# Ordering each engine's instructions by a simulation with DMA queues and semaphores in time: a two-layer hybrid diffusion block

## The chip, the cores and the metric

One NeuronCore of a Trainium2 chip. TensorE (PE) multiplies, VectorE (DVE) and ScalarE (ACT) do the elementwise work, GpSimd (POOL) a little of it, and SyncE (SP) issues most of the loads. Each engine has its own instruction stream and takes it in the order in which it was written; an instruction whose operand is not there waits, and with it all that stands behind it on its engine. The metric is the device time of one execution in microseconds; the span of the profiled execution runs from its first to its last instruction.

## What is computed

Two layers act on 256 tokens `x` and 256 context tokens `ctx`, with 1024 features. In each, a half feed-forward block, a mixer and another half feed-forward block are added to the residual stream, all modulated by vectors made from `c` and `c_ctx`. All is in float32.

```python
def half_ffn(h, shift, scale, gate, g, wi, wo):
    return h + 0.5 * gate * swiglu(modulate(rms_norm(h, g), shift, scale), wi, wo)

def hybrid_layer(x, ctx, c, c_ctx, p, last):
    mod_x = (jax.nn.silu(c) @ p['ada_w'] + p['ada_b'])[:, None, :]
    ...
    x = half_ffn(x, sx[0], sx[1], sx[2], p['ffn1_norm'], p['ffn1_wi'], p['ffn1_wo'])
    ctx = half_ffn(ctx, sc[0], sc[1], sc[2], p['ffn1_norm'], p['ffn1_wi'], p['ffn1_wo'])
    u_x = modulate(rms_norm(x, p['mix_norm']), sx[3], sx[4]) @ p['w_in']
    ...
    x = x + sx[5] * mix_tokens(u_x, rows, dirs_x, states_x, p)
    x = half_ffn(x, sx[6], sx[7], sx[8], p['ffn2_norm'], p['ffn2_wi'], p['ffn2_wo'])
    if not last:
        ctx = ctx + sc[5] * mix_tokens(u_c, None, dirs_c, states_c, p)
        ctx = half_ffn(ctx, sc[6], sc[7], sc[8], p['ffn2_norm'], p['ffn2_wi'], p['ffn2_wo'])
    return x, ctx
```

`mix_tokens` joins four mixers (pooling, a long convolution by transforms, a gated linear attention with chunks, a gated short convolution) and multiplies by `w_out`. After two layers `x` is normalized once more.

## The kernel before, in words

Features lie on the 128 partitions in eight tiles `x` of 128 x 512 (256 tokens of `x`, 256 of `ctx`); the second layer's last stages run on 256 tokens alone. TensorE multiplies fp32 values as pairs of a rounded high part and a remainder: `split` (L171, L172) makes them, the cast to the high part on ScalarE (`whi` of a weight, `yh` of a normed input, `ah` of a modulation weight), the subtraction that gives the low part on VectorE (`wlo`, `yl`, `al`). `mm3` makes three matmuls of each product (L183 high by high, L184 and L185 high by low).

Three places matter below.

*The modulation vectors at the start.* `ada_pe` takes a slab of 512 columns of `ada_w` in eight pieces `adaw`; some go in as they are (L301), some are split into `ah` and `al` (L298, L299). The sums are copied into `row` by ScalarE (L303), turned by four small matmuls against `sum4` (L306), and written to `mods` by VectorE (L308); L366 makes `gs` of them. The first feed-forward block needs shift and scale, four slabs for eight feature tiles: tiles 0 to 3 need the first two slabs that come in, tiles 4 to 7 the other two. Its first two weight tiles are `whi_599`/`wlo_600` and `whi_607`/`wlo_608`; its normed inputs are `yh_519` to `yh_526`.

*The end of each feed-forward block and mixer, where a norm follows* (`project`, `part`). The last two output tiles are computed one half of the tokens after the other. As soon as the first half is done, `rstd` turns its sums of squares by four small matmuls (L406, L407), `rsqrt_cols` works out 1/rms in about fifteen tiny VectorE steps (L210, L212, L215 and three rounds of L219 and L221), and `bcast` spreads it over the partitions (two `diag` on VectorE, L231; two matmuls, L233). Meanwhile TensorE does the last two parts on the second half of the tokens; VectorE adds each to the residual tiles `x_22` and `x_23` (L487), and ScalarE squares them (L389, summed at L393). Then `norm` makes, tile by tile, `ny` (L427), `yh` (ScalarE, L430) and `yl` (L431), which the next block's first matmuls take. This stands four times in the program with 512 tokens: at 420, 628, 996 and 1370 us of the profiled execution.

*The mixer of the second layer*, at 1405 to 1440 us, where many small steps of four mixers are interleaved by a string of letters (`ORDERS`).

The order of the work is not that in which the program is written. The tile framework records all instructions with priorities, which the program shifts for single pieces (`prio`, `issue_after`), and a scheduler then lays them out engine by engine, going by the priorities and a simulation of when each is ready. Buffers are limited: 2 of `whi` and of `wlo`, 3 of `raw`, 4 PSUM buffers each of `psm` and `psa`, so a split also waits for the matmuls that still read its buffer.

Of the kernel before, what the change touches and what calls it, by code (L numbers as in the profile page):

```python
# [17 lines left out]
P = 128  # L18
# [11 lines left out]
CF = 136  # L30
# [30 lines left out]
class Builder:  # L61
# [58 lines left out]
    def mark(self, *engines):  # L120
        """The last instructions traced for VectorE and for the loads, or for other engines."""
        engines = engines or (mybir.EngineType.DVE, mybir.EngineType.SP)
        found = {}
        for i in reversed(self.nc.cur_bb.bb.instructions):
            if i.engine in engines and i.engine not in found:
                found[i.engine] = i
                if len(found) == len(engines):
                    break
        return found
# [23 lines left out]
    def warm_up(self):  # L153
        """Keeps TensorE busy until its first operands are there: its clock is halved after idling."""
        ps = self.pa((P, P))
# [18 lines left out]
    def stack(self, dst, src, low):  # L174
        """src [96, n], the same rows three times -> the high parts, but for one of the three, which gets the low parts: two
        such stacks, with the low parts in different places, make a product of 32 rows in one pass."""
        self.nc.scalar.copy(dst, src)
        s = slice(32 * low, 32 * low + 32)
# [27 lines left out]
    def rsqrt_cols(self, ps, n):  # L206
        """ps [P, n, 2]: v and -v/2. One after the other column by column, so that the columns' chains overlap."""
# [17 lines left out]
    def bcast(self, r, ntile):  # L225
        """r [tokens, ntile] per token -> PSUM [128, ntile*128], the same on every partition."""
# [47 lines left out]
    def ada_fetch(self, l, slab, pools):  # L274
        """The weights of a slab, by k."""
# [12 lines left out]
    def ada_pe(self, l, slab, ws, split):  # L288
        """The rows of c and c_ctx times the weights: four rows, each vector as its high and its low part, times both
        parts of the weights, for the last split parts of the inner dimension; as it is for the first."""  # L290
# [20 lines left out]
    def ada_group(self, l, chunks, vecs):  # L311
        """Yields after each piece of work."""
# [72 lines left out]
    def sumsq(self, m, lo, n):  # L385
        """Adds the squares of tokens lo..lo+n of feature tile m."""
# [11 lines left out]
    def rstd(self, lo, n):  # L398
        """Each token's 1/rms, tokens on partitions."""
# [11 lines left out]
    def spread(self, lo, r):  # L411
        """The same on every partition."""
# [21 lines left out]
    def scaled(self, l, name):  # L434
        """x times the norm's weights and scale, for products that begin before the norm's factor is there."""
# [18 lines left out]
    def project(self, m, wh, wl, act, gate, T, last):  # L454
        """x[m] += gate * (weights.T @ act); with last, the squares for the norm that follows.
        The last two tiles go one half of the tokens after the other, so that the norm of the first half
        can begin early."""
# [38 lines left out]
    def ffn(self, l, name, T, fill, last=1):  # L496
# [26 lines left out]
        def shifted(w):  # L523
            """What the norm's shift adds, per feature."""
# [14 lines left out]
        def late_act(w, c, rb):  # L539
            """act, for products that the norm's factor and shift are still to be applied to."""  # L540
# [65 lines left out]
    def spectra(self, l):  # L606
        """Yields after each piece of work."""
        nc, t = self.nc, self.t
        # the two halves of the positions lie on the two halves of the partitions
# [77 lines left out]
    def mirror(self, lo, hi, even, odd, i):  # L687
        """The transform (0: cosines, 1: sines) at frequencies f and 255 - f, out of the sums over the even and the odd
        positions: cos and sin at 255 - f are (-1)^n cos and -(-1)^n sin at f."""
# [9 lines left out]
    def mix(self, l, last):  # L699
# [8 lines left out]
        def fm(wg, c, n, TT, lo=0):  # L708
            """Features on partitions: n columns of the group for tokens lo..TT."""
# [24 lines left out]
        def tm(wg, tt):  # L734
            """Tokens on partitions, all columns of the group."""
# [29 lines left out]
        def conv_in():  # L765
            """Conformer convolution: the gated input, positions on partitions."""
# [73 lines left out]
        # output projection  # L840
# [16 lines left out]
    def conv(self, l, cv, nq):  # L857
        """The depthwise convolution by a transform of length 2 * CF (at odd multiples of half its frequency, so that the
        CF frequencies are alike), which the positions and half the taps fit in; then norm and SiLU. The first 128
        frequencies lie on partitions, the CF - 128 further ones at first on the free axis."""  # L860
# [10 lines left out]
        # the filter's transform  # L871
# [12 lines left out]
        # the input's transform, and the product  # L884
# [55 lines left out]
        n = T // P  # L940
# [11 lines left out]
    def hyena(self, l, uc, nq, marks):  # L952
# [13 lines left out]
        def tok(pair):  # L966
            """Positions on partitions, the even ones and the odd ones."""
# [15 lines left out]
        for o in range(2):  # L983
            # at f and at 255 - f: the transform, and its product with the filter's
# [22 lines left out]
            # back: what the cosines and the sines at f weigh for the even positions, and for the odd ones  # L1007
# [54 lines left out]
    def gla(self, l, kk, gg, qq, vv, nq):  # L1062
# [71 lines left out]
        # states: chunk index 0..3 for x, 4..7 for ctx  # L1134
# [28 lines left out]
    def gla_gate(self, l, nq, rr):  # L1163
        """The norm over each head's values, and the gate."""
# [30 lines left out]
    def gla_read(self, seq, ke, qbd, vv, before, blk):  # L1195
# [5 lines left out]
        for cp in range(2):  # L1201
            tt = seq * 2 + cp
            # scores within each chunk: its positions on half of the partitions
# [29 lines left out]
    def finish(self):  # L1233
        """The last norm, with the tokens on partitions."""
# [22 lines left out]
    def run(self):  # L1257
# [32 lines left out]
        def filler(*streams):  # L1290
            """Each stream: pieces a step, first step, generator."""
# [174 lines left out]
```

## Time and profile before

| | us |
|---|---|
| time, median of 3 runs | 1713.38 (1712.46 to 1713.61) |
| span of the profiled execution | 1711.8 |
| TensorE busy | 1687.3 (99%) |
| VectorE busy | 1211.6 (71%) |
| ScalarE busy | 592.2 (35%) |
| DMA, mean share of 16 engines (hardware queue) | 42.3% |

The profile names each group of instructions by line, engine and operation, with `out<-in` by the program's names. Behind a row of the timeline, brackets say how long the engine had been idle and what it waited for. Brackets are left out below about 0.2 us.

### The profile page before, as it was taken

Reading aid. Unit: us, or ns where it says so; the run is one execution under the profiler, and the core shown is the slowest. Engines: PE = TensorE matmul, PEld = TensorE weight load, DVE = VectorE, ACT = ScalarE, POOL = GpSimd, SP = SyncE. Lnnn points to the kernel's source line nnn. Section 1 sums busy time; section 2 is a strip of 40 time slices with the busy share of each in tenths; the row PEclk is TensorE's granted clock in tenths of the full one; section 3 lists DMA queues with packets and bytes.
Section 4 is the critical chain, followed back from the end, with each engine's and each line's share of the span. In section 5 each row is a group of like instructions: output and inputs, shape, how many; then the busy total and the mean of one; then the engine's idle time right before and its main releaser. Section 6 shows DMA issues by size and latency. Waiting matters only on the chain.

```text
span 1711.8 us, 23606 instructions
## 1 busy us (share of the span) xinstructions
PE 1687.3 (99%) x9634; PEld 1441.0 (84%) x9634; DVE 1211.6 (71%) x2106; ACT 592.2 (35%) x766; POOL 34.1 (2%) x61
## 2 busy tenths in 40 slices
PE   8999999999999999999999999999999998999998
PEld 4788888878888898888888898888878897899998
DVE  6799965897675778888669876554464678875454
ACT  6432212333542433221222242221233254554343
POOL 0000000010000000000000000000000000000010
PEclk9999999999999999999999999999999999999999
DMA  9355543542232234545445425444432234344552
GB/s 371 128 200 194 186 172 146 175 164 99 81 112 99 78 141 161 184 164 195 151 147 202 174 77 194 172 160 160 150 124 99 93 129 161 108 159 175 181 195 75
DMA packets 50477, 262.56 MB, mean 153 GB/s; under 512 B 5802, under 2 KB 10736, under 8 KB 27584
## 3 DMA queue, kind: packets, MB, share of 16 engines
q1 hardware_dynamic: 48960, 257.05, 42.3%
q0 software_dynamic: 1408, 4.00, 0.6%
q8 instruction: 75, 1.23, 0.3%
q14 instruction: 34, 0.28, 0.0%
HBM read 257.88 MB, written 3.15 MB: 152 GB/s over the span
## 4 chain that ended last, share of the span: by engine, by line
PE 92%; DVE 3%; ACT 1%; issue 1%; DMA 0%; POOL 0%; DVEq 0%; ACTq 0%; POOLq 0%; SPq 0%
PE psm L183 29%; PE psm L184 28%; PE psm L185 28%; DVE acc L331 1%; ACT whi L171 1%; DVE wlo L172 1%; PE psa L989 1%; PE psa L1048 0%; PE psa L1226 0%; PE psa L1208 0%; PE psa L346 0%; PE psa L1028 0%; PE psa L891 0%; PE psa L1018 0%; PE psa L924 0%
## 5 line engine op out<-in xcount | busy, mean ns | idle before, releaser
L185 PE MATMUL psm<-yh,wlo 128*128 128x512 f32 (+1 forms) x1616 | 570.8, 354 | 1.4 <-DVE wlo L172 1.4
L184 PE MATMUL psm<-yl,whi 128*128 128x512 f32 (+1 forms) x1616 | 571.9, 355 | 0.1
L183 PE MATMUL psm<-yh,whi 128*128 128x512 f32 (+1 forms) x1616 | 570.3, 356 | 1.4 <-DVE glu L786 0.9
L171 ACT CAST whi<-raw 128x2048 fp32r<-128x2048 f32 (+3 forms) x171 | 303.9, 1779 | 598.8 <-PE psm L184 532.2
L172 DVE TENSOR_TENSOR wlo<-raw,whi 128x2048 fp32r<-128x2048 f32 (+3 forms) x171 | 363.8, 2128 | 134.4 <-ACT whi L171 134.0
L183 PEld LDWEIGHTS psm<-yh,whi 128*128 128x128 f32 x1616 | 305.1, 190 | 46.8 <-issue 2.3
L185 PEld LDWEIGHTS psm<-yh,wlo 128*128 128x128 f32 x1616 | 305.9, 189 | 44.8 <-DVE wlo L172 2.0
L184 PEld LDWEIGHTS psm<-yl,whi 128*128 128x128 f32 x1616 | 306.2, 190 | 43.0 <-DVE yl L431 0.8
L331 DVE SCALAR_TENSOR_TENSOR acc<-adaw,cvec,acc 128x512 f32<-128x512 f32 x392 | 274.7, 747 | 2.8
L183 PE MATMUL psm<-hh,whi 128*128 128x512 f32 (+1 forms) x752 | 265.1, 353 | 0.0
L185 PE MATMUL psm<-hh,wlo 128*128 128x512 f32 (+1 forms) x752 | 264.3, 352 | 0.0
L184 PE MATMUL psm<-hl,whi 128*128 128x512 f32 (+1 forms) x752 | 264.3, 351 | 0.0
L185 PEld LDWEIGHTS psm<-hh,wlo 128*128 128x128 f32 x752 | 142.3, 189 | 19.4 <-DVE acc L331 0.8
L184 PEld LDWEIGHTS psm<-hl,whi 128*128 128x128 f32 x752 | 142.3, 189 | 19.2 <-DVE hl L172 0.4
L183 PEld LDWEIGHTS psm<-hh,whi 128*128 128x128 f32 x752 | 142.2, 189 | 18.9 <-issue 0.2
L551 DVE TENSOR_TENSOR sg<-psm,sg 128x512 f32<-128x512 f32 (+1 forms) x90 | 54.4, 606 | 130.2 <-PE psm L185 120.2
L487 DVE SCALAR_TENSOR_TENSOR x<-psm,gt,x 128x256 f32<-128x256 f32 x112 | 50.5, 479 | 115.4 <-PE psm L185 115.3
L550 ACT ACTIVATE sg<-psm 128x512 f32<-128x512 f32 (+1 forms) x90 | 48.0, 533 | 211.6 <-PE psm L185 211.6
L389 ACT ACTIVATE sq<-x 128x512 f32<-128x512 f32 (+1 forms) x64 | 33.1, 522 | 90.4 <-DVE x L487 74.4
L183 PE MATMUL psm<-whi,yh 128*128 128x256 f32 (+1 forms) x200 | 58.2, 295 | 0.6 <-ACT whi L171 0.6
L184 PE MATMUL psm<-wlo,yh 128*128 128x256 f32 (+1 forms) x200 | 58.1, 293 | 0.0
L185 PE MATMUL psm<-whi,yl 128*128 128x256 f32 (+1 forms) x200 | 58.0, 293 | 0.0
(293 smaller groups left out, 1534.6 us busy)
## 6 DMA issues: line engine op xcount, KB each, us to landing
raw<-in_ffn_wi_dram SPq DMA_DIRECT2D x88, 1024.0 KB, 4.8
adaw<-in_ada_w_dram SPq DMA_DIRECT2D x68, 1024.0 KB, 5.0
raw<-in_ffn_wo_dram SPq DMA_DIRECT2D x32, 896.0 KB, 4.4
raw<-in_ffn_wo_dram SPq DMA_DIRECT2D x16, 1024.0 KB, 5.0
raw<-in_w_in_dram SPq DMA_DIRECT2D x14, 1024.0 KB, 4.7
raw<-in_w_out_dram SPq DMA_DIRECT2D x8, 1024.0 KB, 4.9
adaw<-in_ada_w_dram SPq DMA_DIRECT2D x16, 256.0 KB, 7.2
pm<-in_k_pool_dram SPq DMA_DIRECT2D x12, 256.0 KB, 2.8
```

The lines of the kernel that those rows point to most:

```text
L171: self.nc.scalar.copy(hi[:, s], src[:, s])
L172: self.nc.vector.tensor_tensor(lo[:, s], src[:, s], hi[:, s].bitcast(F32), op=ALU.subtract)
L183: mm(ps, lhsT=ah, rhs=bh, start=first, stop=False)
L184: mm(ps, lhsT=ah, rhs=bl, start=False, stop=False)
L185: mm(ps, lhsT=al, rhs=bh, start=False, stop=last)
L331: nc.vector.scalar_tensor_tensor(acc, ws[half][:, k, :], sc, acc, op0=ALU.mult, op1=ALU.add)
L389: nc.scalar.activation(sq, self.x[m][:, lo:lo + n], AF.Square)
L487: nc.vector.scalar_tensor_tensor(self.x[m][:, s], ps[:, v * S - lo:v * S - lo + S], gate[v][:, m:m + 1], self.x[m][:, s], op0=ALU.mult, op ...
L550: nc.scalar.activation(sg, w[2][:, s], AF.Silu)
L551: nc.vector.tensor_tensor(sg, w[3][:, s], sg, op=ALU.mult)
L989: nc.tensor.matmul(ps[par], lhsT=fwd[:, 2 * i + par, :], rhs=cur[par], start=True, stop=True)
```

## The change

One argument is given to the tile framework's context: the scheduler's readiness simulation then models DMA queues and semaphores in time. What the program computes, its instructions, tiles, buffers and priorities stay; the order on the engines differs. Comments and docstrings were also taken out of the file, and the line numbers stay the same.

```diff
-    with tile.TileContext(nc) as tc:
+    with tile.TileContext(nc, schedule_with_timeline_sim=True) as tc:
```

TensorE, VectorE, GpSimd and SyncE have as many instructions as before; ScalarE has two more, both loads of an activation table in the second mixer. Three places show the change. Names carry the numbers of tiles and instructions. First TensorE at the end of the modulation's slabs. `psa_510` is the output of the last slab that tiles 4 to 7 of the first block wait for, `psm_603`, `psm_604`, `psm_613` and `psm_614` are that block's first outputs. Before:

```order
L185 MATMUL psm_604<-yh_521,wlo_600 128x512
L183 MATMUL psm_603<-yh_522,whi_599 128x512
L183 MATMUL psm_604<-yh_522,whi_599 128x512
L306 MATMUL psa_510<-sum_12_126,row_508 128x2 x4
L185 MATMUL psm_614<-yh_519,wlo_608 128x512
L184 MATMUL psm_603<-yl_530,whi_599 128x512
```

and now:

```order
L299 MATMUL psa_459<-al_497,c_10_117 4x512
L298 MATMUL psa_459<-ah_502,c_10_117 4x512
L299 MATMUL psa_459<-al_503,c_10_117 4x512
L306 MATMUL psa_510<-sum_12_126,row_508 128x2 x4
L183 MATMUL psm_603<-yh_523,whi_599 128x512
L183 MATMUL psm_604<-yh_523,whi_599 128x512
L183 MATMUL psm_613<-yh_523,whi_607 128x512
```

`yh_523` is tile 4, the first whose modulation comes out of `psa_510`. Before, 22 rows stand between the last L306 and its first matmul; now none does, and the same rows stand ahead of the L306.

Second, ScalarE in the second slab of the start, whose pieces are `adaw_182` and `adaw_184`. Before:

```order
L171 CAST ah_350<-adaw_182 128x512
L171 CAST ah_356<-adaw_182 128x512
L171 CAST ah_362<-adaw_182 128x512
L171 CAST ah_368<-adaw_182 128x512
L171 CAST ah_374<-adaw_184 128x512
L171 CAST ah_380<-adaw_184 128x512
L171 CAST ah_386<-adaw_184 128x512
L171 CAST ah_392<-adaw_184 128x512
L171 CAST whi_599<-raw_186 128x2048
L303 COPY row_398<-psa_349 4x512
```

and now:

```order
L171 CAST ah_356<-adaw_182 128x512
L171 CAST whi_599<-raw_186 128x2048
L171 CAST ah_362<-adaw_182 128x512
L171 CAST ah_368<-adaw_182 128x512
L171 CAST ah_374<-adaw_184 128x512
L171 CAST ah_380<-adaw_184 128x512
L171 CAST ah_386<-adaw_184 128x512
L171 CAST ah_392<-adaw_184 128x512
L303 COPY row_398<-psa_349 4x512
```

The cast of the first weight tile has moved ahead of the slab's last six casts; VectorE has the matching `wlo_600` ahead of the matching six `al`, where it stood behind all of them.

Third, VectorE at the end of the first mixer (628 us). `x_167` and `x_168` are residual tiles 6 and 7, `psm_5276` and `psm_5334` the second halves of the last two parts, `sm` the steps of 1/rms of the first half, `ny_5419` and the next the first normed tiles. Before:

```order
L219 SCALAR_TENSOR_TENSOR sm_961_5306<-sm_960_5301,sm_956_5292 128x1 x2
L221 SCALAR_TENSOR_TENSOR sm_962_5307<-sm_961_5306,sm_960_5301 128x1
L487 SCALAR_TENSOR_TENSOR x_167<-psm_5276,mods_128,x_167 128x256
L221 SCALAR_TENSOR_TENSOR sm_962_5307<-sm_961_5306,sm_960_5301 128x1
L231 TENSOR_SCALAR diag_5348<-ident_99,sm_962_5307 128x128 x2
L393 SCALAR_TENSOR_TENSOR sq_5049<-sq_5331,sq_5049 128x256
L427 SCALAR_TENSOR_TENSOR ny_5419<-x_161,gs_2946,psa_5347 128x256
```

The steps now begin like this:

```order
L487 SCALAR_TENSOR_TENSOR x_167<-psm_5276,mods_128,x_167 128x256
L393 SCALAR_TENSOR_TENSOR sq_5049<-sq_5331,sq_5049 128x256
L210 TENSOR_SCALAR sm_954_5288<-psa_5283 128x2
L212 TENSOR_SCALAR sm_955_5290<-sm_954_5288 128x2
L215 COPY sm_956_5292<-psa_5283 128x2
```

and end like this:

```order
L219 SCALAR_TENSOR_TENSOR sm_961_5306<-sm_960_5301,sm_956_5292 128x1 x2
L487 SCALAR_TENSOR_TENSOR x_168<-psm_5334,mods_128,x_168 128x256
L221 SCALAR_TENSOR_TENSOR sm_962_5307<-sm_961_5306,sm_960_5301 128x1 x2
L231 TENSOR_SCALAR diag_5348<-ident_99,sm_962_5307 128x128 x2
L172 TENSOR_TENSOR wlo_5494<-raw_5495,whi_5493 128x1024 x2
L427 SCALAR_TENSOR_TENSOR ny_5419<-x_161,gs_2946,psa_5347 128x256
```

The residual add and the sum of squares of tile 6 have moved from the end of the 1/rms steps to ahead of their first; the add of tile 7, which needs TensorE's last matmul of the block, from behind the first `ny` to ahead of the last L221; both halves of the weight's low part `wlo_5494` from behind four `ny` to ahead of the first. On TensorE the two L233 stand behind that last matmul instead of twelve matmuls ahead of it, and on ScalarE both halves of the cast `whi_5493` ahead of the first `yh`. The other three places with 512 tokens (420, 996, 1370 us) have changed alike: at 996 one half of the `wlo` stands ahead of the first `ny` and the other behind the third; at 420 and 1370 one half (1152 columns) ahead of the first `ny` and the other (864) behind it, and the L210 stands between the add and the sum of squares.

## Rows read from the trace of the kernel before

**Rows 1.** The page: busy time by engine, and the chain that ended last by engine.
```profile
PE 1687.3 (99%) x9634; PEld 1441.0 (84%) x9634; DVE 1211.6 (71%) x2106; ACT 592.2 (35%) x766; POOL 34.1 (2%) x61
...
PE 92%; DVE 3%; ACT 1%; issue 1%; DMA 0%; POOL 0%; DVEq 0%; ACTq 0%; POOLq 0%; SPq 0%
```

**Rows 2.** Timeline of VectorE and ScalarE at the start: start, length in us, engine, what.
```profile
23.59 4.97 DVE L172 TENSOR_TENSOR al<-adaw,ah 128x512 fp32r<-128x512 f32 x8 [0.27 <-issue]
29.67 2.29 DVE L172 TENSOR_TENSOR wlo<-raw,whi 128x2048 fp32r<-128x2048 f32 x1 [1.11 <-ACT whi L171]
49.65 1.22 DVE L172 TENSOR_TENSOR wlo<-raw,whi 128x1024 fp32r<-128x1024 f32 x1
53.55 0.23 DVE L308 TENSOR_TENSOR mods<-psa,vec 128x4 f32<-128x4 f32 x2 [2.29 <-PE psa L306]
...
57.07 0.51 ACT L430 ACTIVATE yh<-ny,mods 128x256 fp32r<-128x256 f32 x1 [0.40 <-DVE ny L427]
```

**Rows 3.** Timeline of TensorE at the start.
```profile
39.88 1.05 PE L306 MATMUL psa<-sum,row 4*128 4x2 f32 x8 [0.67 <-ACT row L303]
...
52.47 1.05 PE L306 MATMUL psa<-sum,row 4*128 4x2 f32 x8
...
58.58 0.84 PE L183 MATMUL psm<-yh,whi 128*128 128x512 f32 x3
```

**Rows 4.** Timeline of VectorE at 628 us.
```profile
623.49 0.16 DVE L210 TENSOR_SCALAR sm<-psa 128x2 int32<-128x2 int32 x1 [1.43 <-PE psa L407]
...
625.12 0.35 DVE L219 SCALAR_TENSOR_TENSOR sm<-sm,sm 128x1 f32<-128x1 f32 x2
...
625.45 0.48 DVE L487 SCALAR_TENSOR_TENSOR x<-psm,mods,x 128x256 f32<-128x256 f32 x1
...
625.91 0.48 DVE L231 TENSOR_SCALAR diag<-ident,sm 128x128 f32<-128x128 f32 x2
626.48 0.43 DVE L393 SCALAR_TENSOR_TENSOR sq<-sq,sq 128x256 f32<-128x256 f32 x1
627.15 1.26 DVE L427 SCALAR_TENSOR_TENSOR ny<-x,gs,psa 128x256 f32<-128x256 f32 x3 [0.24 <-PE psa L233]
...
629.55 1.22 DVE L172 TENSOR_TENSOR wlo<-raw,whi 128x1024 fp32r<-128x1024 f32 x1
```

**Rows 5.** Timeline of ScalarE and TensorE at 628 us.
```profile
627.66 0.51 ACT L430 ACTIVATE yh<-ny,mods 128x256 fp32r<-128x256 f32 x1 [1.22 <-DVE ny L427]
...
628.52 0.48 PE L183 MATMUL psm<-yh,whi 128*128 128x256 f32 x2
```

**Rows 6.** Timeline of VectorE and TensorE at 996 us.
```profile
993.96 0.43 DVE L393 SCALAR_TENSOR_TENSOR sq<-sq,sq 128x256 f32<-128x256 f32 x1
...
996.01 0.48 PE L183 MATMUL psm<-yh,whi 128*128 128x256 f32 x2
```

**Rows 7.** Timeline of VectorE and TensorE at 420 us.
```profile
418.56 0.43 DVE L393 SCALAR_TENSOR_TENSOR sq<-sq,sq 128x256 f32<-128x256 f32 x1
...
421.87 2.33 DVE L172 TENSOR_TENSOR wlo<-raw,whi 128x1152 fp32r<-128x1152 f32 x2
...
420.75 0.36 PE L183 MATMUL psm<-yh,whi 128*128 128x256 f32 x1
...
421.89 0.53 PE L183 MATMUL psm<-whi,yh 128*128 128x288 f32 x2 [0.30 <-ACT whi L171]
423.02 0.38 PE L407 MATMUL psa<-mean,sq 128*128 128x2 f32 x2 [0.60 <-ACT sq L389]
...
423.71 0.38 PE L183 MATMUL psm<-yh,whi 128*128 128x256 f32 x1
```

**Rows 8.** Stretches: us, busy time (count) of PE, PEld, DVE, ACT, POOL, granted TensorE clock, DMA share, GB/s.
```profile
424.00:427.40 3.40, 3.40 (x17) 3.40 (x17) 3.40 (x18) 0.94 (x3) 0.00 (x0) 0.51 0.66 231
1419.00:1426.00 7.00, 4.07 (x30) 3.46 (x30) 6.89 (x12) 6.42 (x9) 0.00 (x0) 1.00 0.00 0
1426.00:1440.00 14.00, 11.78 (x133) 9.78 (x132) 11.03 (x23) 6.91 (x15) 1.05 (x2) 1.00 0.79 277
```

## The prediction

> **What bounds the kernel now.** I read the page first, then the chain of waits, then the timeline stage by stage. The page shows TensorE busy for 1687.3 of 1711.8 us, and 92% of the chain that ended last runs through it [rows 1]. No other engine is near its limit over the whole: VectorE is busy 71%, ScalarE 35%. So the matmuls' own work is fixed, and an order can move only the time in which TensorE waits: 1711.8 - 1687.3 = 24.5 us at the two ends and in gaps are all that a better order could take out, while a worse one can add without such a limit. The places to look at are therefore those where TensorE works through its last ready matmul while other engines prepare the next operands: the start, the four norms at full width, and the second mixer. In the long stretches of the feed-forward blocks splits, loads and matmuls overlap by many microseconds in both orders, and I cost the moves there at nothing; what hides them is the matmuls of a whole weight tile, and if that cover were gone a split of 2.29 us [rows 2] would show.
>
> [...] The trace has TensorE's weight loads busy for 1441.0 us, 84% [rows 1]. [...]
>
> **The start: +6.6 us.** Two steps. First, the split of the first weight tile goes ahead of six of the second slab's pieces. Before, VectorE's eight `al` run in one piece from 23.59 to 28.56, and `wlo_600` follows at 29.67 with 2.29 us [rows 2]; now those 2.29 us stand inside. One half of the next weight tile's low part, 1.22 us, which ran at 49.65 [rows 2], also goes ahead of the last slab's pieces that the first feed-forward matmul waits for. TensorE has nothing else to do there: it already waited 0.67 us for a `row` at 39.88 [rows 3]. The delay is at least 2.3 (the first move alone) and at most 2.29 + 1.22 = 3.5; I take 2.8, as the 0.67 of waiting takes up the rest. Second, the last L306. Before, it ran at 52.47 to 53.52 in the middle of ready matmuls; `mods`, `gs`, `ny` and `yh` followed from 53.55, and the `yh` that the matmul at 58.58 needs was there at 57.07 + 0.51 = 57.58 [rows 2, 3]: 4.1 us from L306's end, all hidden behind 22 rows of matmuls. Now these rows stand ahead of L306, and the very next matmul needs that `yh`. So TensorE waits out the whole chain. VectorE has one `yl` less inside it, so 3.8 rather than 4.1. Sum 2.8 + 3.8 = 6.6, from 2.3 + 3.8 = 6.1 to 3.5 + 4.1 = 7.6. What is late next is nothing: the same matmuls are done on either side of row 123.
>
> **The norm at 628 us: +4.5 us.** Before, 1/rms of the first half runs from 623.49, beside the last parts, and the first `yh` is there just as the last matmul ends; the next block's first matmul starts at 628.52 without a gap [rows 4, 5]. Now the chain is this. The steps begin behind the sum of squares of tile 6, which ends at 626.48 + 0.43 = 626.91. From L210 to the last L219 they take 625.12 + 0.35 - 623.49 = 1.98. Then the add of tile 7 (its operand, from the last matmul, is there by then), an L221 and the two `diag`: before, an add, an L221 and the two `diag` took from 625.45 to 625.91 + 0.48, that is 0.94; with 0.07 for the other L221, which overlaps its neighbours, 1.01. That is 626.91 + 1.98 + 1.01 = 629.90. Two halves of `wlo` at 1.22 make 632.34, and from the start of `ny` to the end of `yh` it is 627.66 + 0.51 - 627.15 = 1.02 [rows 4, 5], so 633.36; the matmul follows 628.52 - 628.17 = 0.35 later, at 633.7. In its place TensorE has only the six small statistics matmuls to do, which before came later and took 423.71 - 423.02 = 0.69 at the like place [rows 7]. So 633.7 - 628.5 - 0.7 = 4.5. The move of the two L233 behind the last matmul adds nothing to that, since their `diag` comes later still.
>
> **The norm at 996 us: +3.9.** The sum of squares ends at 994.39 [rows 6]. The same steps give 994.39 + 1.98 + 1.01 = 997.38, and one half of `wlo` 998.6; the first matmul is at 998.6 + 1.02 + 0.35 = 999.97, against 996.01 [rows 6]: 3.96 - 0.69 = 3.3. The second `wlo` half stands between the third `ny` and the first `yl`, so the fifth matmul waits once more: 998.6 + 1.26 (three `ny`) + 1.22 + 0.48 (a `yl`, as long as a `ny`) = 1001.5, while the four matmuls ahead of it end at about 1000.9. +0.6, so 3.9.
>
> **The norms at 420 and 1370 us: +2.3 each.** At 420 the sum of squares ends at 418.99 [rows 7]; only the L210 is past by then, so 1.98 less about 0.2 remain. 418.99 + 1.78 + 1.01 = 421.78; the larger half of `wlo` takes 1152/2016 of 2.33 = 1.33, so 423.11; + 1.02 + 0.35 = 424.48. Against 420.75 that is 3.73, less 0.69 = 3.0. About 0.2 comes from the other half, and the gaps of 0.30 and 0.60 that TensorE had there [rows 7] go, since what it waited for now comes early: 3.0 + 0.2 - 0.9 = 2.3. The place at 1370 us shows the same rows and two like gaps.
>
> **The second mixer and the rest: 0.** Between 1419 and 1440 us TensorE idles for 7.00 - 4.07 + 14.00 - 11.78 = 5.15 us [rows 8]. The new order fills some of these waits (a wait for a `wlo` goes, matmuls stand ahead of another) and makes the mixer's vector chain later by two table loads; piece by piece I find TensorE back at the same work 0 to 0.5 us later. I take 0. The first mixer is reordered by up to seventy rows; its waits are not to be read from the trace of before, and the nearest bound is the 5.15 us of the second: from -1 (there is little idle time there to win) to +5.
>
> **The clock: +1.7.** [...] But the 5.15 us between 1419 and 1440 left the clock at 1.00 [rows 8]. [...]
>
> **Sum.** 6.6 + 4.5 + 3.9 + 2.3 + 2.3 + 0 + 1.7 = 21.3. The profiled execution's span is 1711.8, the median of the runs 1713.38, 1.6 more; the same 1.6 is kept: 1713.4 + 21.3 = 1734.7.
>
> **Rivals.** [...] *The norms are paid back*: the splits that are pulled ahead would have to run a few microseconds later anyway, and if the matmuls behind then wait for nothing, VectorE's lead makes up the loss; only the start remains: 1713.4 + 6.6 = 1720. Against it: TensorE had almost no waits behind these places that could be saved, 0.9 us at 420. *Faster through the second mixer*: if its new order takes away all of the 5.15 us of waits there, and the norms and the start are hidden, the time is 1713.4 - 5.2 = 1708. It decides only if all other places together cost under 5.2 us, which the start alone exceeds by my working. *The order on the chip makes no difference*: the waits named do not bind because the chain starts earlier than I think, above all if the add of tile 6 is ready long before; then 1713. Against it, the sum of squares of that tile ends at 626.91 because its operand comes from TensorE, not because VectorE was late.
>
> **How the numbers follow.** My forecast has 0.66, the slow clock everywhere 0.14, paid back 0.08, faster 0.05, no difference 0.07. The single terms' bounds (start 6.1 to 7.6, first mixer -1 to +5, clock 0 to 5.1, the norms within 1.5 each way) put my own case between 1729 and 1744. The range goes from 1719, which takes in the norms paid back, to 1743; 0.12 lie with the two cases below it, and the few above 1743 make up the rest of 2 in 10. A measurement of this kernel can tell about 0.2%, 3.4 us, from no change: faster 0.05, same 0.07, slower 0.88.
>
> **What would show it.** In the changed kernel's timeline TensorE should idle 3.5 to 4.5 us ahead of its first matmul on `yh_523` (around 61 to 65 us), with `yh` or `ny` as releaser; it should idle about 5, 4, 3 and 3 us at the norms, each between the last L185 of the block and the first L183 on a `yh`, with VectorE busy through it and a `wlo` ahead of the first `ny`. TensorE's busy time should be as before but for slow stretches; the windows behind the new gaps show whether the granted clock is 0.5. The forecast is wrong if the gaps at the norms are under 1 us, if the first mixer shows new waits of more than 5 us, or if the first feed-forward matmul does not come later.

## The result

The changed kernel takes 1793.3 us (median of 4 runs, 1789.4 to 1794.1) against 1712.9 beside it: a ratio of 1.046, interval 1.045 to 1.048. It is slower by 80 us, where I had forecast 21, with 1743 as the upper end.

The page of the changed kernel, span and busy time by engine, against [rows 1]:

```profile
span 1792.3 us, 23628 instructions
...
PE 1719.3 (96%) x9634; PEld 1464.6 (82%) x9634; DVE 1213.2 (68%) x2106; ACT 594.9 (33%) x768; POOL 34.1 (2%) x61
```

TensorE has the same 9634 matmuls and is busy 32.0 us longer (1719.3 against 1687.3), and it waits 48.5 us longer (73.0 against 24.5). VectorE and ScalarE are busy as long as before, within 3 us. So there are two things to find: where TensorE waits, and why the same matmuls take 32 us more.

To see where, both programs are cut after the same number of rows on TensorE. Stretches of before, in order: start, norm at 420, first mixer, its end with the norm at 628, norm at 996, norm at 1370, second mixer with the norm behind it (columns: span, busy time and count of PE, PEld, DVE, ACT, POOL, granted clock, DMA share, GB/s):

```profile
0.98:79.89 78.91, 72.40 (x322) 46.59 (x323) 57.09 (x130) 41.79 (x70) 1.71 (x6) 0.94 0.67 256
414.58:433.82 19.24, 18.34 (x132) 17.73 (x132) 15.90 (x61) 7.76 (x16) 1.19 (x3) 0.91 0.19 67
433.82:597.77 163.95, 163.76 (x1176) 136.33 (x1175) 110.69 (x203) 67.57 (x106) 2.11 (x4) 1.00 0.27 95
597.77:640.68 42.91, 42.88 (x283) 39.23 (x282) 31.20 (x81) 16.79 (x27) 0.00 (x0) 1.00 0.35 129
985.33:1011.53 26.20, 26.16 (x214) 25.57 (x213) 23.36 (x74) 10.93 (x24) 0.00 (x0) 1.00 0.24 82
1357.97:1383.38 25.41, 24.50 (x184) 23.90 (x183) 19.48 (x67) 9.55 (x20) 0.00 (x0) 0.93 0.25 90
1383.38:1536.41 153.03, 145.32 (x1255) 133.54 (x1253) 119.03 (x260) 82.12 (x143) 1.05 (x2) 1.00 0.41 143
```

and the same stretches of the changed kernel:

```profile
0.98:92.83 91.85, 77.10 (x322) 51.62 (x323) 57.23 (x130) 41.85 (x70) 1.73 (x6) 0.87 0.57 220
...
428.92:451.06 22.14, 19.78 (x135) 18.98 (x133) 15.25 (x59) 7.73 (x16) 1.19 (x3) 0.85 0.17 58
451.06:642.08 191.02, 174.30 (x1176) 141.67 (x1175) 109.22 (x199) 67.03 (x106) 2.10 (x4) 0.96 0.24 82
642.08:692.53 50.45, 46.15 (x283) 41.64 (x282) 35.06 (x90) 19.11 (x30) 0.00 (x0) 0.93 0.32 126
...
1037.05:1067.70 30.65, 28.70 (x214) 28.01 (x213) 23.31 (x75) 11.22 (x25) 0.00 (x0) 0.89 0.19 70
...
1415.24:1442.32 27.08, 24.64 (x185) 23.92 (x183) 19.38 (x67) 10.03 (x21) 0.00 (x0) 0.94 0.25 85
1442.32:1615.24 172.92, 151.65 (x1255) 139.79 (x1253) 119.45 (x260) 83.05 (x142) 1.05 (x2) 0.94 0.36 127
```

Minus before, the second column, the length of each stretch, is +12.9 (start), +2.9, +27.1 (first mixer), +7.5, +4.5, +1.7 and +19.9 (second mixer). The long feed-forward stretches between them differ by 3 us in all. The third column, TensorE's busy time, is longer by 4.7 of the start's 12.9, 10.5 of the first mixer's 27.1 and 6.3 of the second's 19.9. Most of that, though not all, goes with a slow clock, by an estimate from the clock column: a granted clock of 0.96 over 191.02 us, where it was 1.00, is (1 - 0.96) x 191.02 = 7.6 us of full speed, against the first mixer's 10.5. The mixers, which I had put at nought, hold 47 us.

TensorE's longest waits in the mixers of the changed kernel (timeline; in brackets how long it had waited, and for what):

```profile
511.95 0.66 PE L1111 MATMUL psa<-ident,kexp 128*128 128x128 f32 x4 [3.12 <-DVE kexp L1107]
...
534.29 0.56 PE L1226 MATMUL psa<-blk,v 128*64 128x128 f32 x4 [4.01 <-DVE blk L1214]
...
600.77 1.13 PE L1056 MATMUL psa<-pl,pw 128*128 128x512 f32 x2 [2.39 <-ACT pl L1052]
...
616.09 1.71 PE L1048 MATMUL psa<-pm,up 128*64 128x256 f32 x4 [2.36 <-DMA pm<-in_k_pool_dram]
...
1483.69 1.11 PE L1111 MATMUL psa<-ident,kexp 128*128 128x128 f32 x4 [3.87 <-DVE kexp L1107]
...
1539.11 1.19 PE L1056 MATMUL psa<-pl,pw 128*128 128x256 f32 x2 [3.09 <-DMA pw<-in_pool_w_dram]
...
1596.52 1.01 PE L534 MATMUL psa<-ones,row 2*128 2x1 f32 x4 [3.24 <-ACT row L531]
```

and three 8 us stretches that begin in such a wait or soon after it:

```profile
514.00:522.00 8.00, 7.61 (x47) 6.53 (x48) 4.05 (x10) 2.27 (x4) 0.34 (x1) 0.57 0.53 199
...
1538.00:1546.00 8.00, 6.89 (x27) 4.94 (x28) 2.09 (x6) 1.48 (x4) 0.00 (x0) 0.57 0.25 82
1596.00:1604.00 8.00, 6.75 (x35) 6.67 (x36) 5.66 (x13) 2.84 (x8) 0.00 (x0) 0.57 0.43 160
```

The clock column reads 0.57 over each. Such a stretch loses 8 x (1 - 0.57) = 3.4 us of full speed, a part of it while TensorE still waits. So six of the seven waits above cost twice, once as idle time and once as slower matmuls at or behind them: the granted clock is 0.57 over 514 to 522, 534 to 538, 616 to 624, 1538 to 1546 and 1596 to 1604 us, and 0.79 over 1483 to 1491. Behind the 2.39 us at 600.77 it is 1.00 (600 to 608 us), and it is back at 1.00 from 522 to 530 us, where TensorE is busy throughout (8.00 us). What a slow stretch does to the matmuls shows at the start: those of 128x512 begin 0.43 us apart where the clock is 0.50 (70 to 72 us), and 0.23 us apart where it is 1.00 (60 to 62 us).

### The profile page after: what moved, and what is told of

The parts are those of the page before. It is cut to its first block, busy times and chain, and to the rows that moved or that the text cites. A ratio compares the mean times of both kernels' runs of the same rounds, so it can differ in the third digit from the quotient of the medians.

```text
span 1792.3 us, 23628 instructions
## 1 busy us (share of the span) xinstructions
PE 1719.3 (96%) x9634; PEld 1464.6 (82%) x9634; DVE 1213.2 (68%) x2106; ACT 594.9 (33%) x768; POOL 34.1 (2%) x61
## 5 line engine op out<-in xcount | busy, mean ns | idle before, releaser
L183 PE MATMUL psm<-yh,whi 128*128 128x512 f32 (+1 forms) x1616 | 570.4, 359 | 7.0 <-ACT yh L430 5.3
L185 PE MATMUL psm<-yh,wlo 128*128 128x512 f32 (+1 forms) x1616 | 571.4, 357 | 1.1 <-DVE wlo L172 0.9
L183 PEld LDWEIGHTS psm<-yh,whi 128*128 128x128 f32 x1616 | 308.7, 193 | 51.2 <-ACT yh L430 5.7
L184 PEld LDWEIGHTS psm<-yl,whi 128*128 128x128 f32 x1616 | 309.9, 192 | 46.6 <-DVE yl L431 2.9
L185 PEld LDWEIGHTS psm<-yh,wlo 128*128 128x128 f32 x1616 | 308.4, 192 | 47.6 <-DVE wlo L172 3.1
L185 PE MATMUL psm<-hh,wlo 128*128 128x512 f32 (+1 forms) x752 | 263.2, 351 | 0.7 <-DVE wlo L172 0.7
L183 PE MATMUL psm<-hh,whi 128*128 128x512 f32 (+1 forms) x752 | 262.7, 351 | 0.0
L185 PEld LDWEIGHTS psm<-hh,wlo 128*128 128x128 f32 x752 | 141.9, 189 | 19.9 <-DVE wlo L172 1.1
L183 PEld LDWEIGHTS psm<-hh,whi 128*128 128x128 f32 x752 | 142.1, 189 | 18.7
L183 PE MATMUL psm<-whi,yh 128*128 128x256 f32 (+1 forms) x200 | 59.3, 299 | 0.0
L185 PE MATMUL psm<-whi,yl 128*128 128x256 f32 (+1 forms) x200 | 58.9, 298 | 0.0
L430 ACT ACTIVATE yh<-ny,mods 128x256 fp32r<-128x256 f32 x88 | 41.8, 505 | 39.5 <-DVE ny L427 38.8
```

What stands on the lines that cost most here:

```text
L183: mm(ps, lhsT=ah, rhs=bh, start=first, stop=False)
L184: mm(ps, lhsT=ah, rhs=bl, start=False, stop=False)
L185: mm(ps, lhsT=al, rhs=bh, start=False, stop=last)
L430: nc.scalar.activation(yh[k][:, s], a, AF.Identity, bias=sh)
```

## The experiments

All orders below are fixed by edges that hold each instruction of an engine behind its predecessor, and mean issue order only. They are added once everything is recorded (the unpacking of the lists is left out, and the diffs of most runs below give the edit in words):

```diff
         Builder(ctx, tc, t, out).run()
+        pin(tc)
+
+def pin(tc):
+    nosync = mybir.DependencyInfo(mybir.DependencyClass.NoSync, mybir.DependencyReason.DATA)
+    by = {i.name: i for i in tc.nc.cur_bb.bb.instructions}
+    for names in PIN:
+        for a, b in zip(names, names[1:]):
+            tc.add_manual_dep(by[b], a, nosync, reason="pin")
```

So a stretch can be given one program's order and the rest the other's. "Before" is always the time of the kernel before on the same chip. The changed kernel was measured beside a before of 1712.9; the runs that are set against its 1793.3 have befores between 1712.0 and 1714.0, so such differences are loose by 1 to 2 us.

### Which stretch carries what (e1 to e4, e13)

Only the mixers changed (e1):

```diff
-start, norms, mixers, rest: order of before
+start, norms, rest: order of before; mixers: changed order
```

> The order of before everywhere but in the two mixers (and the norm that follows the second), which stand in the changed order. Theory A, each place carries its own loss: in the changed kernel TensorE falls 27 us further behind between 453 and 616 us and 21 us between 1439 and its end at about 1605, so 1713 + 48 = 1761, between 1750 and 1770. Theory B, the losses hang together (a wait early in the program shifts loads and splits so that later places wait too): a place by itself costs far less, under 1730.

It measured 1761.2 against 1713.8, ratio 1.028 (1.024 to 1.031): +47.3, which is what theory A says. The two activation-table loads that the changed kernel has more are no part of it: they stand at 1371.7 us, ahead of the second mixer, and at 1471.4 there, and e1 has as many ScalarE instructions as before (766).

Only the four norms changed (e2):

```diff
-start, norms, mixers, rest: order of before
+start, mixers, rest: order of before; norms: changed order
```

> The order of before but at the four norms of full width, which stand in the changed order. Theory A: the sum of my four terms, 13.0 us, and as the changed kernel's rows show 13 to 14: 1726. Theory B: under 1718, since the splits that are pulled ahead are paid back once the rest of the order is that of before.

It measured 1727.0, ratio 1.007 (1.005 to 1.010): +13.1. The stretches of the four norms in e2, cut after the same rows as those of before above:

```profile
414.85:436.91 22.06, 19.70 (x133) 18.87 (x132) 15.96 (x61) 8.06 (x16) 1.18 (x3) 0.85 0.17 58
600.88:647.81 46.93, 44.34 (x284) 40.64 (x283) 32.50 (x84) 17.67 (x28) 0.00 (x0) 0.96 0.36 135
992.45:1022.67 30.22, 27.66 (x215) 26.98 (x214) 23.08 (x74) 11.16 (x24) 0.00 (x0) 0.94 0.19 71
1369.09:1396.80 27.71, 25.89 (x185) 25.07 (x184) 19.27 (x66) 9.76 (x20) 0.00 (x0) 0.88 0.24 83
```

They are longer by 2.8, 4.0, 4.0 and 2.3 us, of which 1.4, 1.5, 1.5 and 1.4 are longer busy time.

Only the start changed (e3):

```diff
-start, norms, mixers, rest: order of before
+norms, mixers, rest: order of before; start: changed order
```

> The order of before but in the first 75 us, which stand in the changed order. Theory A: 12 to 13 us, as the changed kernel is 12.5 us behind at that point: 1725 to 1726; of my terms only 6.6 us, that is 1720, if the slow clock came from elsewhere. Theory B: the start is the cause of later waits too, so over 1735.

It measured 1725.6, ratio 1.006 (1.004 to 1.009): +11.7.

All but the mixers changed (e4):

```diff
-start, norms, mixers, rest: changed order
+start, norms, rest: changed order; mixers: order of before
```

> The changed order everywhere but in the two mixers (and the norm that follows the second), which stand in the order of before. Theory A: 1793 - 48 = 1745, between 1736 and 1756. Theory B: above 1765, since what comes before the mixers makes them wait.

It measured 1746.2, ratio 1.019 (1.015 to 1.023): 47.1 below the changed kernel, as much as e1 is above before.

The rest alone changed (e13):

```diff
-start, norms, mixers, rest: order of before
+start, norms, mixers: order of before; rest: changed order
```

> The order of before, but all that lies outside the start, the four norms and the two mixers in the changed order. Theory A, as 47.3, 13.1 and 11.7 us of 79.5 are found: 7.4 are left, 1721. If the parts meet at their edges (a wait that is cut off from its cause), less: 1714 to 1717.

It measured 1717.4, ratio 1.002 (1.001 to 1.003): +3.4. No run fixes the whole order of before, so what the added edges cost by themselves is not measured; e13, fixed throughout, leaves little room for it. The four parts give 47.3 + 13.1 + 11.7 + 3.4 = 75.5 of the 80 us. The loss sits in its places, and theory B, that an early wait brings on the later ones, falls. Some 5 us remain at the edges or in the spread of the runs.

### Which engine's order in the mixers (e5, e6, e12, e14)

VectorE and ScalarE in the changed order, TensorE and the loads laid out anew around them by the scheduler of before (e5):

```diff
-mixers: all engines in the order of before
+mixers: VectorE, ScalarE in the changed order; TensorE, SyncE free
```

> The order of before; in the two mixers VectorE and ScalarE stand in the changed order, while TensorE and the loads there are laid out by the scheduler of before around them. Theory C, long work that is not urgent stands ahead of the steps that TensorE waits for on VectorE and ScalarE, so that these two orders carry the loss: 1745 to 1762, most of the 47 us. Theory D, TensorE's own order is the cause (matmuls that wait stand ahead of matmuls that are ready), and TensorE can fill the time if its rows may move: under 1728.

It measured 1759.3, ratio 1.027 (1.025 to 1.029): +45.6, as theory C has it.

The mirror of it (e6):

```diff
-mixers: all engines in the order of before
+mixers: TensorE in the changed order; VectorE, ScalarE, SyncE free
```

> The order of before; in the two mixers TensorE stands in the changed order, while VectorE, ScalarE and the loads there are laid out by the scheduler of before around it. Theory C: under 1728. Theory D: 1745 to 1762.

It measured 1778.1, ratio 1.038 (1.036 to 1.040): +64.5, more than all engines together in e1. That is outside what either theory said. Two of its waits (timeline of TensorE in e6):

```profile
641.32 0.55 PE L183 MATMUL psm<-mh,whi 128*128 128x256 f32 x1 [4.42 <-DVE x L487]
...
1582.80 1.01 PE L534 MATMUL psa<-ones,row 2*128 2x1 f32 x4 [7.07 <-ACT row L531]
```

Here the two engines, free to choose, made TensorE wait longer than in the order that belongs with it. So e5 doesn't show that VectorE and ScalarE are *the* cause. What the pair shows is that the changed orders can't be mended by giving the other engines a free hand under the scheduler of before: each order alone costs about as much as all of them, or more.

The loads alone (e12), and everything but the loads (e14):

```diff
-mixers: all engines in the order of before
+mixers: SyncE in the changed order; TensorE, VectorE, ScalarE in the order of before
```

> The order of before; in the two mixers SyncE's loads alone stand in the changed order. If late loads are a cause of their own, some 6 us, as the waits for loads in the changed kernel are 0.60, 2.36 and 3.09 us: 1718 to 1722. If the loads are late only because the engines that free their buffers are late, 1712 to 1716.

It measured 1730.5, ratio 1.010 (1.008 to 1.011): +16.5, more than either expectation. Two waits hold most of it (timeline of TensorE in e12):

```profile
581.62 1.97 PE L1048 MATMUL psa<-pm,up 128*64 128x256 f32 x4 [7.76 <-DMA pm<-in_k_pool_dram]
...
1486.32 1.19 PE L1056 MATMUL psa<-pl,pw 128*128 128x256 f32 x2 [3.94 <-DMA pw<-in_pool_w_dram]
```

These are 11.7 us of waiting for two small loads (256 and 64 KB), with a slow clock at both (0.63 over 581 to 590 us, 0.66 over 1484 to 1494). The `pm` is issued at 576.45, right behind a 1 MB load at 576.06 that had waited 8.7 us for a `wlo` to free its buffer; before, all `pm` loads of this mixer are issued by 566.80. Cut after the same rows, the first mixer is 11.9 us longer in this execution and the second 6.8. What was left open after these runs was whether that adds to the other engines' share.

```diff
-mixers: all engines in the changed order
+mixers: TensorE, VectorE, ScalarE in the changed order; SyncE in the order of before
```

> As e1 (both mixers in the changed order, all else as before: 1761.2), but SyncE's loads in the mixers stand in the order of before. If the loads' 16.5 us (e12) add to what VectorE, ScalarE and TensorE cost, 1743 to 1747. If the loads' waits lie inside waits that the other engines make anyway, 1755 to 1762.

It measured 1755.2 against 1712.0, ratio 1.024 (1.022 to 1.027): +43.1, against 47.3 with the changed loads. Of the loads' 16.5 us only about 4 come on top here: in e1 TensorE waits 2.05 and 3.13 us for a `pm` and a `pw` where it waits 7.76 and 3.94 in e12, as other waits have made it later by then. So in the mixers the shares of the engines don't add, while the shares of the stretches do.

### Single causes taken away from the changed kernel (e7, e10, e11, e15)

The weight splits held back (e7):

```diff
+for a, b in zip(order_of_before, order_of_before[1:]):
+    if is_weight_split(b):
+        tc.add_manual_dep(by[b], a, nosync, reason="pin")
```

> The changed scheduler; the only edges added hold each cast and each subtraction of a weight tile (342 instructions) behind the instruction that stood ahead of it in the order of before, all else is free. If the splits are the work that stands in the way, the norms lose most of their 13 us, the start 3 to 8 and the mixers a good half: 1793 falls to 1750 to 1765. If the other steps that moved ahead (residual adds, products of the attention, statistics) do the same harm, it stays above 1778.

It measured 1778.9, ratio 1.038 (1.036 to 1.040): 14.4 below the changed kernel, at the edge of "the others do as much harm". Holding the splits back wins less than a fifth of the loss. What they carry by themselves isn't shown, as the rest was free to move and holding them makes waits of its own: three for a `whi` or `wlo` of 1.1 to 1.5 us between 416 and 487 us in its timeline, and a wait of 5.50 us at 523.85 that is longer than any of the changed kernel. Cut after the same rows, the first mixer takes 177.6 us (191.0 in the changed kernel, 164.0 before), so half of its loss goes; the start takes 86.7 (91.9 and 78.9), with its wait of 3.88 us still there, and the second mixer 169.8 (172.9 and 153.0). The stretches of the four norms are 20.2 us longer than before together, where they are 16.6 longer in the changed kernel: held splits did not mend them.

Three small loads first (e10). SyncE in the changed kernel, and in before, at the pooling weight `pw` of the second mixer:

```profile
1533.86 0.34 SPq L447 DMA_DIRECT2D raw<-in_ffn_wi_dram  x1
1534.31 0.37 SPq L1054 DMA_DIRECT2D pw<-in_pool_w_dram  x1
```

```profile
1468.87 0.34 SPq L1054 DMA_DIRECT2D pw<-in_pool_w_dram  x1
...
1470.92 0.34 SPq L447 DMA_DIRECT2D raw<-in_ffn_wi_dram  x1
```

```diff
-raw_2166 (1 MB), pw_2029, pm_2035, pm_2036
+pw_2029, pm_2035, pm_2036, raw_2166 (1 MB)
```

> The changed order, but three small loads of the second mixer (one of the pooling weights, two of the pooling matrices) stand ahead of the 1 MB load of a later weight tile on SyncE. If TensorE's wait of 3.09 us at 1536 us comes from the small load's place in SyncE's queue, the wait goes, and with it the slow clock behind it (0.50 to 0.79 for 8 us, 3.4 us lost, some of it in the wait): 1793.3 less 3 to 6, that is 1787 to 1790. If something else is late there as well, 1792 to 1794.

It measured 1789.6 (1787.1 to 1790.9), 3.7 below the changed kernel's 1793.3. The two ranges of runs meet (1790.9 and 1789.4), so the size is loose, but the wait of 3.09 us for `pw` is gone from the timeline; what stands there is 0.95 us for a `pm`. SyncE in e10:

```profile
1524.45 0.89 SPq L1046 DMA_DIRECT2D pm<-in_k_pool_dram  x2
1530.45 0.34 SPq L1054 DMA_DIRECT2D pw<-in_pool_w_dram  x1
```

SyncE now pauses 5.1 us ahead of `pw` (1525.34 to 1530.45), as it paused 5.0 us ahead of the 1 MB load in the changed kernel (1528.83 to 1533.86). So `pw` was not late because the large load held up the queue. It landed late: behind the large load its matmul was released 4.8 us after its issue, ahead of it the `pw` loads land in 1.7 us (the list of DMA issues of e10, 1530 to 1536 us). Ten small loads first (e15):

```diff
+ten small loads (5 of the pooling, 5 of transforms and filters): ahead of the weight loads that they led before
```

> The changed order, but ten small loads on SyncE (five of them those of the pooling, the others of transforms and filters) stand ahead of the large weight loads that they stood ahead of in the order of before. If small loads behind large ones carry the loads' share, the waits of 0.60, 2.36 and 3.09 us and the slow clock behind them go: 1793.3 less 8 to 14, 1779 to 1785. If the buffers that these loads fill come free late, so that they can't start sooner, 1787 to 1793, no more than e10.

It measured 1784.8 (1783.4 to 1790.9) against 1712.0, ratio 1.043 (1.040 to 1.045): 8.5 below the changed kernel, though one of the four runs lies within its range. Of the three waits for loads 0.83 us remain. In the changed kernel `pm` loads of the first mixer, too, are issued right behind 1 MB loads (at 603.93 and 608.19 us, 0.65 and 0.43 behind).

The attention's chain first (e11). VectorE in the changed kernel ahead of the wait at 511.95 us:

```profile
504.81 2.77 DVE L1123 SCALAR_TENSOR_TENSOR qbd<-q,eb 32x512 f32<-32x512 f32 x4
507.61 2.29 DVE L172 TENSOR_TENSOR wlo<-raw,whi 128x2048 fp32r<-128x2048 f32 x1
509.82 0.69 DVE L1104 TENSOR_TENSOR kexp<-cum 128x512 f32<-128x512 f32 x1
```

Its input, `cum`, was there at 501.28; four more L1123 stand above these. The edit moves the L1104 ahead of the eight L1123, and the second L1107 and the L1117 only ahead of the `wlo`, not of the L1123 as the expectation has it:

```diff
 L1107 kexp_682
-L1102 dec_681, L1123 qbd_686 x4, L1102 dec_688, L1123 qbd_693 x4
-L172 wlo_788, L1104 kexp_689, L1117 ke_685, L1107 kexp_689
+L1104 kexp_689, L1102 dec_681, L1123 qbd_686 x4, L1102 dec_688, L1123 qbd_693 x4
+L1107 kexp_689, L1117 ke_685, L172 wlo_788
```

> The changed order, but on VectorE in the first mixer three short steps of the attention's chain (L1104, L1107, L1117) stand ahead of the eight products (L1123) and the weight's low part that ran before them. If these long steps make TensorE wait (3.12 us at 509 us), the wait goes to under 0.5 us, and the slow clock behind it goes at least in part (0.50 to 0.79 for 8 us): 1793.3 less 3 to 6, 1787 to 1790. If the wait only moves to the next step of the chain, 1791 to 1794.

It measured 1794.3 (1791.5 to 1795.4), the same time as the changed kernel. The wait of 3.12 us is gone from the timeline. In its place stand shorter waits further down the same chain, and the next long one is as long as ever (TensorE, and two stretches with the clock):

```profile
512.61 1.11 PE L1149 MATMUL psa<-v,kdt 64*32 64x64 f32 x24 [1.29 <-DVE st L1153]
...
532.78 0.69 PE L1226 MATMUL psa<-blk,v 128*64 128x128 f32 x4 [4.01 <-DVE blk L1214]
```

```profile
514.00:522.00 8.00, 7.54 (x48) 6.25 (x48) 3.46 (x9) 1.96 (x4) 0.00 (x0) 0.79 0.80 311
532.00:540.00 8.00, 6.29 (x82) 4.78 (x84) 6.97 (x13) 0.00 (x0) 0.00 (x0) 0.50 0.40 131
```

TensorE reaches the L1226 1.5 us earlier (532.78 against 534.29), and the clock behind the first place recovers (0.79 instead of 0.57); but behind the second the whole 8 us now run at 0.50, where the changed kernel was slow from 534 to 538 only (0.57). What was won is given back there. The edit itself has a part in that: the `wlo` now runs from 510.13 to 512.42, right ahead of the L1153 that the wait of 1.29 us is for. So one wait of a chain with several was not worth its length here; whether an order without that `wlo` would have kept the gain was not tried.

### The clock by itself (e9)

The order of e3, and on TensorE matmuls on constants in the wait ahead of tile 4 (constants written out):

```diff
+        self.slabs = getattr(self, "slabs", 0) + 1
+        if self.slabs == 4:
+            fill = self.pa((P, P))
+            for i in range(14):
+                nc.tensor.matmul(fill, lhsT=self.ones, rhs=self.ones, start=True, stop=True)
```

> The order of e3 (only the first 75 us changed), with 14 further matmuls of 128 columns on constants (some 3 us of work, their result unused) on TensorE in the wait ahead of the first matmul on tile 4. If the slow clock that follows that wait (0.50 to 0.58 for 68 to 74 us in the changed kernel) comes from the idle time itself, it goes: 1725.6 less 2.5 to 3.5, that is 1722 to 1723. If it comes from something else, 1725 to 1727.

It measured 1725.3 (1725.0 to 1727.6) against e3's 1725.6 (1723.9 to 1726.0). The same stretch in e3 and in e9:

```profile
66.00:74.00 8.00, 4.79 (x15) 3.81 (x16) 6.16 (x16) 3.63 (x8) 0.00 (x0) 0.79 0.00 0
```

```profile
66.00:74.00 8.00, 7.45 (x39) 6.02 (x38) 4.90 (x13) 2.66 (x6) 0.00 (x0) 1.00 0.00 0
...
67.95 1.20 PE L185 MATMUL psm<-yh,whi 128*128 128x512 f32 x4 [0.55 <-ACT yh L437]
```

(The added lines shift the numbers: L185 is e3's L183.) The filling matmuls end 0.55 us short of the wait's end. The four matmuls behind take 1.20 us, where the changed kernel took 2.07 (from 68.58 us) for the same ones. Where this wait is left idle, the clock is 0.57 over 66 to 74 us in the changed kernel, 0.79 in e3, and 0.50 over 68 to 74 us in e15; it is 1.00 over 66 to 74 us in e9. So in these profiles the slow stretch goes with the idle time; over all runs, the mean clock is 0.991 to 0.992 in e3 and 0.992 to 0.994 in e9. Yet the time of the whole is no different within what the runs tell: here the stretch costs only 8 x (1 - 0.79) = 1.7 us, less than I expected, since e3's was shorter than the changed kernel's. That the clock is worth as much in the total is not shown. Behind shorter waits the slow stretch also differs with one and the same order: at the norm of 420 us the clock is 0.50 over 424 to 426 and 0.67 over 426 to 428 us before, but 0.79 over 422 to 424 and 0.50 over 424 to 430 us in e1, which keeps that order.

No version beat the kernel before; the best of what these runs point to is its own order.

## Why the prediction was wrong, step by step

**The sign and the method: right.** TensorE's matmuls are the same, and the loss is waits at places where its next operand is late, with slow matmuls behind them (a granted clock of 0.57 to 0.79 at the six longest).

**The norms: right in sum, by luck in part.** I had 4.5 + 3.9 + 2.3 + 2.3 = 13.0, all of it waiting, and e2 measured 13.1. But of the 13.2 us of its four stretches 5.7 are longer busy time, mostly, by an estimate from the clock column (0.85, 0.96, 0.94 and 0.88; before 0.91, 1.00, 1.00 and 0.93), the slow clock that I had counted elsewhere, and only 7.5 are waiting: the waits were put too high by about as much as the clock took. The sequence is there as worked out. VectorE at 628, now 672 us:

```profile
672.73 0.42 DVE L393 SCALAR_TENSOR_TENSOR sq<-sq,sq 128x256 f32<-128x256 f32 x1 [0.54 <-ACT sq L389]
...
675.46 0.48 DVE L487 SCALAR_TENSOR_TENSOR x<-psm,mods,x 128x256 f32<-128x256 f32 x1
...
676.05 0.48 DVE L231 TENSOR_SCALAR diag<-ident,sm 128x128 f32<-128x128 f32 x2
676.45 2.35 DVE L172 TENSOR_TENSOR wlo<-raw,whi 128x1024 fp32r<-128x1024 f32 x2
678.72 1.26 DVE L427 SCALAR_TENSOR_TENSOR ny<-x,gs,psa 128x256 f32<-128x256 f32 x3
```

and TensorE:

```profile
675.15 0.28 PE L185 MATMUL psm<-mh,wlo 128*128 128x256 f32 x1
676.39 0.49 PE L233 MATMUL psa<-diag,ones 128*128 128x128 f32 x2 [0.96 <-DVE diag L231]
...
679.79 1.22 PE L183 MATMUL psm<-yh,whi 128*128 128x256 f32 x4 [0.73 <-ACT yh L430]
```

From the last L185's end to the first L183 it is 679.79 - 675.43 = 4.4 us. I had 5.2 (633.7 against 628.5), of which statistics fill 0.7. From the end of the sum of squares to that L183 the chain is nearly as long as I had it (679.79 - 673.15 = 6.6 against 633.7 - 626.9 = 6.8). The rest is that it begins earlier: the sum of squares now ends 2.3 us ahead of the end of the block's last matmul (before, 1.6), and I had left it in its old place. At 996 us in the changed kernel 2.5 of the 4.5 us are longer matmuls and 1.9 idle.

**The start: little more than half its size.** I had 6.6; e3 measured 11.7. The second step was right: 3.8 forecast, and

```profile
68.58 2.07 PE L183 MATMUL psm<-yh,whi 128*128 128x512 f32 x4 [3.87 <-ACT yh L430]
```

with `yh` as the releaser. The first step was the one mis-sized. Instead of 2.8, the L306 of 39.88 [rows 3] starts at 45.04, 5.2 later. Two pairs of waits (1.07 and 2.02 us for an `ah` and an `al` of the second slab, 1.11 and 1.77 us in the third) stand where the splits were put, and the clock is at 0.50 from 44 to 48 us. The 0.67 us of waiting for `row`, which I let take up a part of the delay, is still there (0.66 us ahead of 45.04). In all, 4.7 us of the start's 12.9 in the changed kernel are longer busy time.

**The mixers: the step that failed.** I put them at 0, with +5 as the upper bound for the first, taken from the 5.15 us that TensorE idled in the second before [rows 8]. The changed order of the two mixers alone costs 47.3 us (e1); in the changed kernel the first is 27.1 us longer and the second 19.9. The 5.15 us is no bound: idle time of the old order says what a better order could win, not what a worse one can lose. What I should have counted is in the two orders and the old durations. On VectorE five instructions moved ahead of the second L1093, a step of the attention's chain (two `wlo` of 2.29, an L803 and an L805 of 0.74 and an L1104 of 0.69: 6.75 us), and a third `wlo` ahead of the L1104 behind it; on TensorE 48 short rows, 0.12 us apart, moved ahead of the L1111 of 511.95, some 5.8 us of cover. That these moves make the wait is argued, not shown; holding all splits back took away half of the first mixer's loss (e7). I read the second mixer piece by piece to "0 to 0.5 later" and left out that SyncE's small loads stand behind a large one; the loads' order alone makes the second mixer 6.8 us longer and the first 11.9 (e12). How the 47 us divide among engines can't be said, as their shares overlap (e5, e6, e14), and which moves make them stays open.

**The clock: the chance was on the wrong side.** I counted 1.7 us, one new slow stretch at three places (the start, 628 and 996 us) at 3.40 x (1 - 0.51) [rows 8], and at most 5.1. No run shows the 1.7 as the price of such a place, nor the 5.1: in the changed kernel all three have a slow stretch, 0.57 over 66 to 74 us, 0.58 over 678 to 686 and 0.58 over 1050 to 1058, each a loss of some 3.4 us by 8 x (1 - 0.58). So the slow clock everywhere, to which I gave 0.14, came true at these places at twice that price, but the total did not follow from it, as it had nothing for the mixers. The row that misled me, 1.00 through 1419 to 1440 us [rows 8], had no single wait over 1.62 us; the six waits of 3.09 to 4.01 us in the changed kernel each had slow rows at or behind them (0.57 to 0.79).

## What to carry to other kernels

Where a scheduler reorders a kernel bound by one engine, list for each step that this engine waits for the instructions that moved ahead of it on its own engine or queue, and add up their old durations; do this above all in stretches of short, interleaved steps, and don't bound what can't be read by the idle time of before. No run here shows how near such a sum comes. A wait of some microseconds on TensorE can have a second price, slower matmuls behind it: here each of the six waits of over 3 us had it, with a granted clock of 0.57 to 0.79 over 4 to 8 us at or behind it. To find where a reordering loses, give one stretch after another the other order: the stretches' shares added up here to 75.5 of 80 us, while the engines' shares within a stretch did not add at all.

## What was not expected of the hardware

TensorE's busy time grew by 32.0 us for the same matmuls, two fifths of the whole loss, beside about 48 us of added waiting. The mean granted clock fell from 0.994 to 0.975: (1 - 0.975) x 1792.3 - (1 - 0.994) x 1711.8 = 34.5 us of full speed lost, some of them while TensorE waited. With 14 matmuls on constants in one wait of 3.9 us, TensorE idled for 0.55 us at its end, and the granted clock was 1.00 over 66 to 74 us (e9), where it was 0.79 with the wait left idle (e3). And the 64 KB load of `pw` issued at 1534.31 us, 0.45 behind a 1 MB load, released its matmul only at 1539.11, 4.8 us after its issue; for the same loads the list of DMA issues of before gives 1.8 us from issue to landing.
